# An inference step with attention scores as three float32r products, attention steps in pairs and later table requests

## Chip, cores and metric

The kernel runs on one core of a Trainium2 chip. The metric is the device time of one execution in microseconds (us). It is given as the median of several executions, and one further execution was recorded by the profiler. TensorE does the matrix products, VectorE (DVE), ScalarE (ACT) and GpSimd (POOL) the elementwise work. SyncE (SP) requests most transfers, GpSimd's queue requests the attention tables.

## The reference

One step of a two-layer model on 128 context tokens and 256 latent tokens (a grid of 4 rows by 64), model width 1024. Each layer, cut to its lines:

```python
h = rmsnorm(x, g1) * (1 + sc1) + sh1
u = h @ w_in
u_pool, u_q, u_k, u_v, u_x, u_y, u_g = jnp.split(u, SPLITS, axis=-1)
y_a = pool_branch(u_pool, pool_w, pool_scale)
y_b = attn_fn(q, k, v).reshape(b, l, ATTN_W)
hf, hb = rglru_branch(u_x, conv_w, conv_b, wa, ba, wx, bx, lam, h0f, h0b)
y_c = (hf + hb) * gelu(u_y)
proj = einsum('blnw,nwd->blnd', stack([y_a, y_b, y_c]), w_branch)
x = x + gt1 * (sum(gates * proj) @ w_out)
x = x + gt2 * ((silu(fg) * fu) @ w_ff_out)
```

Attention has 8 heads of 64. A context query sees the 128 context keys. A latent query has one softmax over its grid neighbourhood, with a learned bias and a column mask, together with 128 cached context keys:

```python
s_lat = einsum(qg, kb) * ATTN_SCALE + bias
s_lat = jnp.where(mask, s_lat, NEG_INF)
s_ctx = einsum(qg, ck) * ATTN_SCALE
p = softmax(concatenate([s_lat, s_ctx]))
```

The shifts, scales and gates come from SiLU(cond) @ w_mod + b_mod, six vectors of 1024 per layer (the modulation).

## The kernel before

All 384 tokens are the columns of every large product. Every large operand is split into two float32r halves, hi = round(x) and lo = x - hi, and a product is the sum hi·hi + lo·hi + hi·lo (`mm3`, L340 to L344). ACT makes the hi half of a weight tile (L305), DVE the lo half (L314); an activation is split likewise by `split_g` (L359, L362) or `split_from`.

The program is one list of jobs written out by hand. A `job` (L408) takes its weight tiles, runs their products, calls `tick()` (which moves on the pending generators of earlier evacuations, among them those in `lazy`), calls `side_step()` (one step of a side branch) and pushes its own evacuation. `after()` then adds a rate `modr[0]` times the job's units and does one modulation step for each whole number reached (`mod_step`, one DVE product-and-sum of 128x1024, L262). The rates of layer l are the rows of `MR` (L49). The first three belong to the branches in the order in which they run, which are pool, LRU and attention (b = 0, 2, 1), the fourth to the stage between pool and LRU, in which `values_job` and `qkv(p)` for p = 0 to 3 make values, queries and keys.

Attention is a side branch (`branch_attn`, L691). Its units are (p, hh, qt): a pair of heads p, a head of the pair hh, and a query block qt of 128 latent queries; with qt = 0 come the 128 context queries as well. There are 16 units a layer. It is a loop over steps i, one step for each job: at even i the scores of two units (L702, two heads, each on 64 of the 128 rows of TensorE's array), at i + 1 the first part of the softmax (`soft_a`, whose DVE step is L718), then `soft_b`, `soft_c` (its DVE step is L735), transposes (L744), their copy out of PSUM (`evac`), and at odd i the products with the values of a pair of units (L774, L779). A score tile is three products in fp32: queries by 256 keys, by the 128 cached keys (`ckv`), and for qt = 0 the context queries by the context keys. `mask_bias` (L686) adds the column mask to the two bias tables of a pair, `load_attn` (L671) requests bias tables and cached keys and values for a pair, and `ev_qkv` (L846) moves queries and keys out of PSUM in fp32.

At the start of layer 0, `start()` (L935 to L1177) works on the first modulation vectors. Near its end `fb` products (L1157) are turned by seven small `mt` products (L1168) into the shift of the first tiles, whose evacuations go into `lazy`. The jobs 19 to 23 follow (job 19 makes the last LRU tile, 20 to 23 the gates `gy` of that branch), and then `pool_proj` (L583), four products of pooled tiles `pd` whose halves are `pdh` and `pdl`. The LRU tiles are `xp`, and their convolution `cv` has one ACT step (L596) and three DVE steps (L599).

Of the kernel before, what the change touches and what calls it, by code (L numbers as in the profile page):

```python
# [20 lines left out]
NT = NC_ + NL  # L21
# [24 lines left out]

WN = (8, 1, 1, 3)

MR = ((0.7, 2.3, 1.8, 0.3, 1.3, 1.1, 0.1), (0.6, 0.8, 0.8, 0.3, 1.3, 0.7, 0))  # L49


def chunk_order():
# [38 lines left out]
def emit(ctx, tc, A, outs):  # L91
# [594 lines left out]
    def mask_bias(y, p):  # L686
        for h in (2 * p, 2 * p + 1):
            t = y["bias", h][:, :384].rearrange("p (r c) -> p r c", r=6)
            V.tensor_tensor(t, t, cmask.unsqueeze(1).to_broadcast([128, 6, 64]), op=OP.add)

    def branch_attn(l, y):  # L691
        def scores(p, qt):

            ss = [psum("sc") for _ in range(2)]
            q, k, ck = y["q", p], y["k", p], y["ckv", p]
            parts = [(slice(0, 256), k, slice(128, 384), 128 + qt * 128), (slice(256, 384), ck, slice(0, 128), 128 + qt * 128)]
            if qt == 0:
                parts.append((slice(384, 512), k, slice(0, 128), 0))
            for o_, m, c_, qo in parts:
                for hh in range(2):  # L700
                    r = slice(64 * hh, 64 * hh + 64)
                    T.matmul(ss[hh][:, o_], q[r, qo:qo + 128], m[r, c_], start=True, stop=True)  # L702
            return ss

        def soft_a(s, h, qt):
            pr, m = heap("pr"), small("m")
            bo = 128 if qt == 0 else 0
            n = 2 if qt == 0 else 1
            prs = [pr, m]
            S.activation(pr[:, 256:384], s[:, 256:384], AF.Copy)  # L710
            if qt == 0:
                pc = heap("pc")
                S.activation(pc[:, :128], s[:, 384:512], AF.Copy)
                prs.append(pc)
            V.tensor_reduce(m[:, 0:n], s[:, 256:256 + n * 128].rearrange("p (a c) -> p a c", a=n),
                            axis=AX.X, op=OP.max)
            r4 = dict(r=4)
            V.tensor_tensor_reduce(pr[:, 0:256].rearrange("p (r c) -> p r c", **r4),  # L718
                                   s[:, 0:256].rearrange("p (r c) -> p r c", **r4),
                                   y["bias", h][:, bo:bo + 256].rearrange("p (r c) -> p r c", **r4)[:, :, ::-1],  # L720
                                   op0=OP.add, op1=OP.max, scale=1.0, scalar=m[:, 0:1], accum_out=m[:, 0:1])
            V.tensor_scalar(m[:, 2:2 + n], m[:, 0:n], -1.0, None, op0=OP.mult)
            return prs

        def soft_b(prs):
            m = prs[1]
            S.activation(prs[0][:, :384], prs[0][:, :384], AF.Exp, bias=m[:, 2:3], accum_out=m[:, 4:5])
            if len(prs) == 3:
                S.activation(prs[2][:, :128], prs[2][:, :128], AF.Exp, bias=m[:, 3:4], accum_out=m[:, 5:6])

        def soft_c(prs):
            n = len(prs) - 1
            m = prs[1]
            V.reciprocal(m[:, 6:6 + n], m[:, 4:4 + n])
            V.tensor_scalar(prs[0][:, :384], prs[0][:, :384], m[:, 6:7], None, op0=OP.mult)  # L735
            if n == 2:
                V.tensor_scalar(prs[2][:, :128], prs[2][:, :128], m[:, 7:8], None, op0=OP.mult)

        def transp(prs):
            tp = psum("tp")  # L740
            n = len(prs) + 1
            for j in range(n):
                src = prs[0][:, j * 128:(j + 1) * 128] if j < 3 else prs[2][:, :128]
                T.transpose(tp[:, j * 128:(j + 1) * 128], src, ident)  # L744
            return tp, n

        def evac(tp, n):
            pt = heap("pt")
            pts = [pt]
            S.activation(pt[:, :384], tp[:, :384], AF.Copy)  # L750
            if n == 4:
                pc = heap("ptc")
                V.tensor_copy(pc[:, :128], tp[:, 384:512])
                pts.append(pc)
            return pts

        units = [(p, hh, qt) for p in range(4) for qt in range(2) for hh in range(2)]
        pr, o, pend = {}, {}, []
        nu = len(units)

        def begin(p):
            mask_bias(y, p)

        def values(j):
            p, _, qt = units[2 * j]
            ts = [pr.pop(2 * j), pr.pop(2 * j + 1)]
            vv, cv = y["vv", p], y["ckv", p]
            if qt == 0:
                o[p] = psum("o")
            for jj in range(-1 if qt == 0 else 0, 3):  # L770
                for hh in range(2):
                    rows = slice(hh * 64, hh * 64 + 64)
                    if jj < 0:
                        T.matmul(o[p][rows, 0:128], vv[:, rows], ts[hh][1][:, 0:128], start=True, stop=True,  # L774
                                 skip_group_check=True)
                        continue
                    wv = cv[:, 128 + hh * 64:192 + hh * 64] if jj == 2 else \
                        vv[:, 128 * (jj + 1) + hh * 64:128 * (jj + 1) + hh * 64 + 64]
                    T.matmul(o[p][rows, 128 + qt * 128:256 + qt * 128], wv, ts[hh][0][:, jj * 128:(jj + 1) * 128],  # L779
                             start=jj == 0, stop=jj == 2, skip_group_check=True)  # L780

        i = 0
        while i < nu + 7 or pend:
            if i < nu and ("k", units[i][0]) not in y:
                yield
                continue
            for g in list(pend):
                if next(g, "end") == "end":
                    pend.remove(g)
            if 0 <= i - 1 < nu:  # L790
                p, hh, qt = units[i - 1]
                pr[i - 1] = soft_a(pr[i - 1], 2 * p + hh, qt)
            if 0 <= i - 2 < nu:
                soft_b(pr[i - 2])
            if 0 <= i - 3 < nu:
                soft_c(pr[i - 3])
            if 0 <= i - 5 < nu:
                pr[i - 5] = evac(*pr[i - 5])
            if i % 2 and 0 <= i - 7 < nu:
                values((i - 7) // 2)  # L800
            if 0 <= i - 4 < nu:
                pr[i - 4] = transp(pr[i - 4])
            if i % 2 == 0 and i < nu:
                p, hh, qt = units[i]
                if qt == 0:
                    begin(p)
                pr[i], pr[i + 1] = scores(p, qt)
            if i % 4 == 2 and 0 <= i - 10 < nu:
                p = (i - 10) // 4
                pend.append(split_g(putter(y, (1, p)), o.pop(p)[:, :NT], name="yb"))  # L810
                next(pend[-1])
                for key in (("vv", p), ("ckv", p), ("bias", 2 * p), ("bias", 2 * p + 1), ("q", p), ("k", p)):
                    y.pop(key)
            i += 1
            yield
# [29 lines left out]

    def ev_qkv(l, kind, p, y):  # L846
        def f(ps):
            t = heap(kind)
            S.activation(t[:, :NT], ps[:, :NT], AF.Copy, scale=0.125 if kind == "q" else 1.0)
            if kind != "q":  # L850
                G.dma_start(out=outs[kind][l, p], in_=t[:, 0:128])
            y[kind, p] = t
            return
            yield
        return f
# [79 lines left out]
    def start(y):  # L935
# [227 lines left out]
        for hf in range(3):  # L1163
            n = 384 if hf < 2 else 128
            S.activation(sb[hf][:, :n], fb[hf][:, :n], AF.Copy)
        ps = psum("mt")
        for g in range(7):
            T.matmul(ps[:, 2 * g:2 * g + 2], sb[g // 3][:, (g % 3) * 128:(g % 3) * 128 + 128], sel,  # L1168
                     start=True, stop=True)
        shw = cp.tile([128, 14], F32, name="shw0")  # L1170
        V.tensor_copy(shw, ps[:, 0:14])
        evs = [ev_pool(0, g, y) for g in range(4)] + [ev_ux(0, c, y) for c in range(3)]
        for g, ev in enumerate(evs):
            lazy.append(ev((un[g], shw[:, 2 * g:2 * g + 2])))
        load_crow()
        w_ahead(0)
        return mv  # L1177

    for l in range(L):
        y = {}  # L1180
        if l == 0:
            mv = start(y)
            todo = [19, 20, 21, 22, 23]
        else:
            mv = first_group(l, 1, [("in", l, m) for m in range(4)], [ev_pool(l, g, y) for g in range(4)], 2)
# [4 lines left out]
            job([[("in", l, m, 8)]], mv, ev, **kw)  # L1190

        for m in todo:
            win(m, ev_pool(l, m, y) if m < 4 else ev_ux(l, m - 16, y) if m < 20 else ev_uy(l, m - 20, y))
        def qkv(p):
            if p < 3:
                load_attn(l, y, p + 1)
            win(4 + p, ev_qkv(l, "q", p, y))
            win(8 + p, ev_qkv(l, "k", p, y))

# [190 lines left out]
```

## Time and profile before

| what | us |
|---|---|
| median of 3 executions | 1232.99 |
| lowest and highest | 1231.52, 1233.26 |
| the profiled execution | 1231.6 |
| its span, first to last instruction | 1229.8 |
| TensorE busy | 1219.8 |
| DVE busy | 888.3 |
| ACT busy | 598.4 |
| POOL busy | 72.6 |

Of the profiled execution 1.8 us lie around the span. The granted TensorE clock is 0.999 of full speed over the span. A busy time is the union of an engine's instructions, so a matrix product that has started but waits in the pipeline counts as well. The share of an engine is a mean over stages; the rows further on show single stages.

### The profile page before, as it was taken

To read this page: it belongs to the slowest core of one execution; us is meant where nothing else is said; L and a number is where in the kernel's file an instruction comes from. 1 tells how busy PE (TensorE), PEld (TensorE's weight loads), DVE (VectorE), ACT (ScalarE), POOL (GpSimd) and SP (SyncE) were. 2 spreads that over 40 slices of the span, in tenths; PEclk is the share of its full clock that TensorE was granted. 3 is DMA by queue.
4 is the path that set the end of the run, shared out by engine and by line. 5 is a ranking of instruction groups with operands and counts; after the bars stand their busy time and mean duration, and the time that the engine had idled before them with its cause. 6 is when DMAs were issued, how large, how long until landed. Compare 5 with 4: busy or idle time off the path is not lost.

```text
span 1229.8 us, 19387 instructions
## 1 busy us (share of the span) xinstructions
PE 1219.8 (99%) x7348; PEld 1190.6 (97%) x7348; DVE 888.3 (72%) x1650; ACT 598.4 (49%) x1103; POOL 72.6 (6%) x187
## 2 busy tenths in 40 slices
PE   9999999999999999999999999999999999999997
PEld 7799999899999999999999999999999999999997
DVE  6798698998978887757779668787676785442432
ACT  5587845544455333333357576564344743332321
POOL 0000150000200000010000013100010000000000
PEclk9999999999999999999999999999999999999999
DMA  9635684466626666645643457632553355333321
GB/s 346 256 132 190 187 177 134 147 209 217 202 98 207 235 226 212 202 150 182 214 138 113 158 167 190 142 118 100 172 197 129 119 207 171 131 109 108 115 88 52
DMA packets 63645, 204.30 MB, mean 166 GB/s; under 512 B 7744, under 2 KB 10944, under 8 KB 63424
## 3 DMA queue, kind: packets, MB, share of 16 engines
q1 hardware_dynamic: 60912, 197.56, 48.2%
q0 software_dynamic: 2496, 5.25, 3.5%
q8 instruction: 57, 0.93, 0.3%
q14 instruction: 36, 0.29, 0.1%
q10 hardware_dynamic: 144, 0.26, 0.1%
HBM read 200.41 MB, written 2.63 MB: 165 GB/s over the span
## 4 chain that ended last, share of the span: by engine, by line
PE 58%; issue 22%; DVE 1%; POOL 0%; POOLq 0%; DVEq 0%
PE ps L342 18%; PE ps L344 18%; PE ps L343 18%; PE tp L744 1%; PE o L779 1%; PE sc L702 1%; PE vt L1210 0%; PE vt L1211 0%; PE vt L1212 0%; DVE junk L262 0%; DVE wlo L314 0%; PE o L774 0%; DVE pr L718 0%; PE st L473 0%; DVE yo L1306 0%
## 5 line engine op out<-in xcount | busy, mean ns | idle before, releaser
L342 PE MATMUL ps<-hh,whi 128*128 128x384 f32 x1256 | 422.2, 336 | 0.0
L344 PE MATMUL ps<-hl,whi 128*128 128x384 f32 x1256 | 419.9, 334 | 0.0
L343 PE MATMUL ps<-hh,wlo 128*128 128x384 f32 x1256 | 419.7, 334 | 0.0
L314 DVE TENSOR_TENSOR wlo<-raw,whi 128x1024 fp32r<-128x1024 f32 (+2 forms) x296 | 322.8, 1115 | 21.7 <-ACT whi L305 21.7
L305 ACT ACTIVATE whi<-raw 128x1024 fp32r<-128x1024 f32 (+2 forms) x296 | 279.8, 970 | 97.3 <-PE ps L344 59.8
L342 PEld LDWEIGHTS ps<-hh,whi 128*128 128x128 f32 x1256 | 235.7, 188 | 2.4 <-issue 0.3
L343 PEld LDWEIGHTS ps<-hh,wlo 128*128 128x128 f32 x1256 | 235.8, 188 | 0.1
L344 PEld LDWEIGHTS ps<-hl,whi 128*128 128x128 f32 x1256 | 235.7, 188 | 0.0
L262 DVE SCALAR_TENSOR_TENSOR junk<-wm,crow 128x1024 bf16<-128x1024 f32 x160 | 195.4, 1221 | 27.0 <-DMA wm<-in_wm 25.0
L909 ACT ACTIVATE ft<-ps 128x384 f32<-128x384 f32 x40 | 19.7, 493 | 202.8 <-PE ps L344 202.8
L342 PE MATMUL ps<-svh,whi 128*128 128x384 f32 x352 | 117.6, 334 | 0.0
L343 PE MATMUL ps<-svh,wlo 128*128 128x384 f32 x352 | 117.6, 334 | 0.0
L344 PE MATMUL ps<-svl,whi 128*128 128x384 f32 x352 | 117.6, 334 | 0.0
L894 DVE SCALAR_TENSOR_TENSOR x<-ps,modv,x 128x128 f32<-128x128 f32 x64 | 23.7, 412 | 81.6 <-PE ps L344 81.5
L911 DVE TENSOR_TENSOR ft<-ft,ps 128x384 f32<-128x384 f32 x40 | 22.1, 552 | 80.7 <-ACT ft L909 80.7
L872 ACT ACTIVATE tg<-ps 128x384 f32<-128x384 f32 x48 | 23.4, 489 | 89.0 <-PE ps L344 88.2
L342 PEld LDWEIGHTS ps<-svh,whi 128*128 128x128 f32 x352 | 66.1, 188 | 0.0
L343 PEld LDWEIGHTS ps<-svh,wlo 128*128 128x128 f32 x352 | 66.1, 188 | 0.0
L344 PEld LDWEIGHTS ps<-svl,whi 128*128 128x128 f32 x352 | 66.1, 188 | 0.0
L881 DVE SCALAR_TENSOR_TENSOR tg<-tg,ps 128x384 f32<-128x384 f32 x48 | 26.4, 551 | 44.0 <-PE ps L344 43.9
L453 ACT ACTIVATE sq<-x 128x384 f32<-128x384 f32 x40 | 20.1, 513 | 66.4 <-DVE x L894 66.4
L342 PE MATMUL ps<-mgh,whi 128*128 128x384 f32 x128 | 42.8, 334 | 0.0
(242 smaller groups left out, 1770.7 us busy)
## 6 DMA issues: line engine op xcount, KB each, us to landing
raw<-in_fi SPq DMA_DIRECT2D x88, 512.0 KB, 4.3
raw<-in_in SPq DMA_DIRECT2D x82, 512.0 KB, 3.9
wm<-in_wm SPq DMA_DIRECT2D x80, 512.0 KB, 4.3
raw<-in_fo SPq DMA_DIRECT2D x32, 512.0 KB, 4.6
raw<-in_br SPq DMA_DIRECT2D x48, 256.0 KB, 2.7
w<-in_wm SPq DMA_DIRECT2D x16, 512.0 KB, 7.0
raw<-in_wo SPq DMA_DIRECT2D x16, 512.0 KB, 3.7
raw<-in_fo SPq DMA_DIRECT2D x16, 384.0 KB, 3.1
```

The costliest lines, as they stand in the source:

```text
L262: V.scalar_tensor_tensor(j, t, 0.5, crow[:, s], op0=OP.mult, op1=OP.mult, accum_out=modv[l][:, comp, d, s:s + 1])
L305: S.activation(hi[:, :nk], r[:, :nk], AF.Copy)
L314: V.tensor_tensor(lo[:, :nk], r[:, :nk], hi[:, :nk].bitcast(F32), op=OP.subtract)
L342: T.matmul(ps[:, :n], hi[:, k], mv[0][:, :n], start=start, stop=False)
L343: T.matmul(ps[:, :n], lo[:, k], mv[0][:, :n], start=False, stop=False)
L344: T.matmul(ps[:, :n], hi[:, k], mv[1][:, :n], start=False, stop=stop)
L453: S.activation(sq[:, :NT], xt[d], AF.Square)
L872: S.activation(t[:, :NT], ps[:, :NT], AF.Tanh, scale=0.5)
L881: V.scalar_tensor_tensor(t[:, :NT], t[:, :NT], 1.0, ps[:, :NT], op0=OP.add, op1=OP.mult)
L894: V.scalar_tensor_tensor(xt[d][:, o:o + n], ps[:, o:o + n], modv[l][:, comp, d, s:s + 1], xt[d][:, o:o + n], op0=OP.mult, op1=OP.add)
L909: S.activation(t[:, :NT], pg[:, :NT], AF.Silu)
L911: V.tensor_tensor(t[:, :NT], t[:, :NT], pu[:, :NT], op=OP.mult)
```

## The change

Five edits. The scores become three float32r products of query and key halves: `ev_qkv` splits queries and keys as they leave PSUM (and copies the context keys to a tile `ko` for the output), and `prep(p)` splits the cached keys on GpSimd into `ck`. The attention loop handles the two units of a pair together at an odd step, transposes, values and then scores, and copies both transposed tiles at an even step. The mask is added by GpSimd. Layer 0's modulation rates are other numbers. The tables of a pair are requested at that pair's predecessor's first scores and no longer in `qkv`, and the seven `mt` products with their evacuations (`rest()`) come one job later.

```diff
-MR = ((0.7, 2.3, 1.8, 0.3, 1.3, 1.1, 0.1), (0.6, 0.8, 0.8, 0.3, 1.3, 0.7, 0))
+MR = ((1.1, 1.9, 1.6, 0.5, 1.3, 1.1, 0.1), (0.6, 0.8, 0.8, 0.3, 1.3, 0.7, 0))
...
-            V.tensor_tensor(t, t, cmask.unsqueeze(1).to_broadcast([128, 6, 64]), op=OP.add)
+            G.tensor_tensor(t, t, cmask.unsqueeze(1).to_broadcast([128, 6, 64]), op=OP.add)
...
-            q, k, ck = y["q", p], y["k", p], y["ckv", p]
+            q, k, ck = y["q", p], y["k", p], y["ck", p]
...
-                for hh in range(2):
-                    r = slice(64 * hh, 64 * hh + 64)
-                    T.matmul(ss[hh][:, o_], q[r, qo:qo + 128], m[r, c_], start=True, stop=True)
+                for a, b in ((0, 0), (1, 0), (0, 1)):
+                    for hh in range(2):
+                        r = slice(64 * hh, 64 * hh + 64)
+                        T.matmul(ss[hh][:, o_], q[a][r, qo:qo + 128], m[b][r, c_], start=a + b == 0, stop=b == 1,
+                                 skip_group_check=True)
...
-        def begin(p):
+        def prep(p):
+
+            t, c = y["ckv", p], heap("ck", F32R)
+            hi, lo = c[:, 0:128], c[:, 128:256]
+            G.tensor_copy(hi, t[:, 0:128])
+            G.tensor_tensor(lo, t[:, 0:128], hi.bitcast(F32), op=OP.subtract)
+            y["ck", p] = (hi, lo)
             mask_bias(y, p)
...
+            if 0 <= i < nu:
+                p, hh, qt = units[i]
+                pr[i] = soft_a(pr[i], 2 * p + hh, qt)
             if 0 <= i - 1 < nu:
-                p, hh, qt = units[i - 1]
-                pr[i - 1] = soft_a(pr[i - 1], 2 * p + hh, qt)
+                soft_b(pr[i - 1])
             if 0 <= i - 2 < nu:
-                soft_b(pr[i - 2])
...
+                soft_c(pr[i - 2])
+            if i % 2 == 0:
+                for u in (i - 6, i - 5):
+                    if 0 <= u < nu:
+                        pr[u] = evac(*pr[u])
+            else:
+                for u in (i - 5, i - 4):
+                    if 0 <= u < nu:
+                        pr[u] = transp(pr[u])
+                if 0 <= i - 7 < nu:
+                    values((i - 7) // 2)
+                if i + 1 < nu:
+                    p, hh, qt = units[i + 1]
+                    if qt == 0 and p < 3:
+                        load_attn(l, y, p + 1)
+                    pr[i + 1], pr[i + 2] = scores(p, qt)
+            if i % 4 == 2 and i < nu and units[i][0] < 3:
+                prep(units[i][0] + 1)
...
-            t = heap(kind)
-            S.activation(t[:, :NT], ps[:, :NT], AF.Copy, scale=0.125 if kind == "q" else 1.0)
-            if kind != "q":
-                G.dma_start(out=outs[kind][l, p], in_=t[:, 0:128])
-            y[kind, p] = t
+            if kind == "k":
+                t = heap("ko")
+                S.activation(t[:, 0:128], ps[:, 0:128], AF.Copy)
+                G.dma_start(out=outs["k"][l, p], in_=t[:, 0:128])
+            y[kind, p] = split_from(ps[:, :NT], scale=0.125 if kind == "q" else 1.0, name=kind)
...
-        ps = psum("mt")
-        for g in range(7):
-            T.matmul(ps[:, 2 * g:2 * g + 2], sb[g // 3][:, (g % 3) * 128:(g % 3) * 128 + 128], sel,
-                     start=True, stop=True)
...
+        def rest():
+            ps = psum("mt")
+            for g in range(7):
+                T.matmul(ps[:, 2 * g:2 * g + 2], sb[g // 3][:, (g % 3) * 128:(g % 3) * 128 + 128], sel,
+                         start=True, stop=True)
...
+            for g, ev in enumerate(evs):
+                lazy.append(ev((un[g], shw[:, 2 * g:2 * g + 2])))
...
+            if m == 20 and l == 0:
+                rest()
...
-            if p < 3:
-                load_attn(l, y, p + 1)
```

TensorE's order at one place of the attention of layer 0, before: the values of a pair run behind a job together with three transposes, and scores follow a job later behind four transposes (`tp`: transposes, `o`: values, `sc`: scores, `ps`: the big products of a job).

```order
L774 MATMUL o<-ptc,vv 64x128 x2
L779 MATMUL o<-pt,vv 64x128 x4
L779 MATMUL o<-pt,ckv 64x128 x2
L744 MATMUL tp<-ident,pr 128x128 x3
L342 MATMUL ps<-ych,whi 128x384
...
L344 MATMUL ps<-ycl,whi 128x384
L744 MATMUL tp<-ident,pr 128x128 x3
L744 MATMUL tp<-ident,pc 128x128
L702 MATMUL sc<-k,q 128x256 x2
L702 MATMUL sc<-ckv,q 128x128 x2
L702 MATMUL sc<-k,q 128x128 x2
```

After, at the place where the same pair's values stand (`kh`, `kl`, `qh`, `ql` are the halves of keys and queries, `ck` those of the cached keys):

```order
L748 MATMUL tp<-ident,pr 128x128 x6
L784 MATMUL o<-ptc,vv 64x128 x2
L789 MATMUL o<-pt,vv 64x128 x4
L789 MATMUL o<-pt,ckv 64x128 x2
L703 MATMUL sc<-kh,qh 128x256 x2
L703 MATMUL sc<-kh,ql 128x256 x2
L703 MATMUL sc<-kl,qh 128x256 x2
L703 MATMUL sc<-ck,qh 128x128 x2
L703 MATMUL sc<-ck,ql 128x128 x2
L703 MATMUL sc<-ck,qh 128x128 x2
L703 MATMUL sc<-kh,qh 128x128 x2
L703 MATMUL sc<-kh,ql 128x128 x2
```

The transposes of two units, the values of a pair and the scores of the next pair now form one block between two jobs, and each score product is there three times. Over a layer there are 19 such blocks of small products before and 12 after.

ACT's order ahead of `pool_proj` in layer 0, before: the hi halves of the last two pooled tiles (`pdh`) stand on either side of the first LRU tile (`xp`, `cv`) and of the last gate (`gy`, job 23).

```order
L305 ACTIVATE whi<-raw 128x1024
L359 ACTIVATE pdh<-pd 128x384
L559 ACTIVATE xp<-un,shw_863 128x128
L559 ACTIVATE xp<-un,shw_863 128x256
L596 ACTIVATE cv<-xp,par 128x386
L840 ACTIVATE gy<-ps 128x384
L359 ACTIVATE pdh<-pd 128x384
```

And after:

```order
L858 ACTIVATE gy<-ps 128x384
L359 ACTIVATE pdh<-pd 128x384
L559 ACTIVATE xp<-un,shw_935 128x128
L559 ACTIVATE xp<-un,shw_935 128x256
L596 ACTIVATE cv<-xp,par 128x386
L359 ACTIVATE pdh<-pd 128x384
```

The last gate now stands ahead of both hi halves, and the whole stretch of the first LRU tile between the two. On DVE the three steps of that tile's convolution stand ahead of the lo half of the last pooled tile, before as after.

## Rows read from the trace of the kernel before

**Rows 1.** The page, part 1: busy us, share of the span, instructions

```profile
PE 1219.8 (99%) x7348; PEld 1190.6 (97%) x7348; DVE 888.3 (72%) x1650; ACT 598.4 (49%) x1103; POOL 72.6 (6%) x187
```

**Rows 2.** TensorE's waits: waiting line, released by, us, times, longest

```profile
PE mt L1168 <- ACT mb L1165: 1.0, 1, 1.0
PE tp L744 <- DVE pr L735: 0.6, 1, 0.6
```

**Rows 3.** Timeline of TensorE in a job of layer 0: start us, us

```profile
68.73 0.33 PE L343 MATMUL ps<-hh,wlo 128*128 128x384 f32 x1
...
71.33 0.33 PE L343 MATMUL ps<-hh,wlo 128*128 128x384 f32 x1
```

**Rows 4.** Timeline of TensorE around one block of scores, layer 1

```profile
764.55 0.34 PE L344 MATMUL ps<-hl,whi 128*128 128x384 f32 x1
764.81 0.70 PE L702 MATMUL sc<-k,q 64*128 64x256 f32 x4
765.35 0.39 PE L702 MATMUL sc<-ckv,q 64*128 64x128 f32 x4
765.57 0.39 PE L702 MATMUL sc<-k,q 64*128 64x128 f32 x4
765.89 0.44 PE L342 MATMUL ps<-hh,whi 128*128 128x384 f32 x1
766.17 0.34 PE L343 MATMUL ps<-hh,wlo 128*128 128x384 f32 x1
```

**Rows 5.** Timeline of TensorE at the `mt` products

```profile
56.49 1.72 PE L1168 MATMUL mt<-sel,mb 128*128 128x2 f32 x14 [1.02 <-ACT mb L1165]
58.07 0.42 PE L342 MATMUL ps<-hh,whi 128*128 128x384 f32 x1
```

**Rows 6.** Timeline of TensorE at transposes, layer 1

```profile
783.70 0.49 PE L744 MATMUL tp<-ident,pr 128*128 128x128 f32 x3
784.03 0.27 PE L744 MATMUL tp<-ident,pc 128*128 128x128 f32 x1
```

**Rows 7.** Timeline of ACT ahead of the pool products, layer 0

```profile
79.16 0.49 ACT L840 ACTIVATE gy<-ps 128x384 f32<-128x384 f32 x1 [0.81 <-PE ps L344]
79.55 0.52 ACT L359 ACTIVATE pdh<-pd 128x384 fp32r<-128x384 f32 x1
79.96 0.80 ACT L559 ACTIVATE xp<-un,shw 128x128 f32<-128x128 f32 x2
80.85 0.71 ACT L596 ACTIVATE cv<-xp,par 128x386 f32<-128x386 f32 x1
```

**Rows 8.** Timeline of DVE in the same stretch

```profile
80.30 0.55 DVE L362 TENSOR_TENSOR pdl<-pd,pdh 128x384 fp32r<-128x384 f32 x1
81.59 2.00 DVE L599 SCALAR_TENSOR_TENSOR cv<-xp,par,cv 128x386 f32<-128x386 f32 x3 [0.74 <-ACT cv L596]
83.51 0.55 DVE L362 TENSOR_TENSOR xcl<-cv,xch 128x386 fp32r<-128x386 f32 x1
```

**Rows 9.** Timeline of TensorE, the last pool product

```profile
80.91 0.44 PE L344 MATMUL ps<-pdl,whi 128*128 128x384 f32 x1
```

**Rows 10.** Windows: us, PE, PEld, DVE, ACT, POOL busy (instructions), clock, DMA share, GB/s

```profile
204.00:264.00 60.00, 59.40 (x433) 54.65 (x431) 57.81 (x145) 32.70 (x84) 0.00 (x0) 1.00 0.48 154
798.00:860.00 62.00, 62.00 (x451) 57.11 (x450) 47.15 (x123) 32.37 (x85) 0.00 (x0) 1.00 0.35 115
```

**Rows 11.** Timeline of TensorE and DVE in one attention step, layer 0

```profile
216.49 0.38 PE L744 MATMUL tp<-ident,pr 128*128 128x128 f32 x2
219.24 0.48 DVE L718 CUSTOM_DVE_ANT_1 pr<-sc,bias,m 128x256 f32<-128x256 f32 x1
```

**Rows 12.** Groups of DVE instructions: count, busy us, mean ns, idle before

```profile
L262 DVE SCALAR_TENSOR_TENSOR junk<-wm,crow 128x1024 bf16<-128x1024 f32 x160 | 195.4, 1221 | 27.0 <-DMA wm<-in_wm 25.0
L689 DVE TENSOR_TENSOR bias<-bias,cmask 128x384 f32<-128x384 f32 x16 | 8.1, 550 | 0.0
```

**Rows 13.** Groups of POOL instructions, as above

```profile
L448 POOL TENSOR_TENSOR xsl<-modv,xsh 128x2 fp32r<-128x2 f32 x24 | 12.7, 529 | 70.5 <-DVE sq L458 52.3 <-PE ps L343 13.2 <-PE ps L344 2.6
```

**Rows 14.** Transfers: issuing queue, count, KB each, median us to landing

```profile
bias<-in_rpb POOLq DMA_DIRECT2D x32, 96.0 KB, 7.4
```

More of the change, by code (lines that the diff above doesn't have):

```diff
@@ L711, in soft_a @@
             if qt == 0:
-                pc = heap("pc")
+                if h % 2 == 0:
+                    y["pc", h // 2] = heap("pc")
+                pc = y["pc", h // 2][:, 128 * (h % 2):128 * (h % 2) + 128]
                 S.activation(pc[:, :128], s[:, 384:512], AF.Copy)
@@ L780, in values @@
                              start=jj == 0, stop=jj == 2, skip_group_check=True)
-        i = 0
+        prep(0)
+        i = -1
         while i < nu + 7 or pend:
-            if i < nu and ("k", units[i][0]) not in y:
+            if i % 2 and i + 1 < nu and ("k", units[i + 1][0]) not in y:
                 yield
@@ L789, in branch_attn @@
                     pend.remove(g)
+            if 0 <= i < nu:
+                p, hh, qt = units[i]
+                pr[i] = soft_a(pr[i], 2 * p + hh, qt)
             if 0 <= i - 1 < nu:
-                p, hh, qt = units[i - 1]
-                pr[i - 1] = soft_a(pr[i - 1], 2 * p + hh, qt)
+                soft_b(pr[i - 1])
             if 0 <= i - 2 < nu:
-                soft_b(pr[i - 2])
[L795 to L807, printed above, removed]
+                soft_c(pr[i - 2])
[16 more added lines that the diff above has]
+                prep(units[i][0] + 1)
             if i % 4 == 2 and 0 <= i - 10 < nu:
@@ L811, in branch_attn @@
                 next(pend[-1])
-                for key in (("vv", p), ("ckv", p), ("bias", 2 * p), ("bias", 2 * p + 1), ("q", p), ("k", p)):
+                for key in (("vv", p), ("ckv", p), ("ck", p), ("bias", 2 * p), ("bias", 2 * p + 1), ("q", p), ("k", p)):
                     y.pop(key)
@@ L1165, in start @@
             S.activation(sb[hf][:, :n], fb[hf][:, :n], AF.Copy)
-        ps = psum("mt")
-        for g in range(7):
-            T.matmul(ps[:, 2 * g:2 * g + 2], sb[g // 3][:, (g % 3) * 128:(g % 3) * 128 + 128], sel,
-                     start=True, stop=True)
[L1170 to L1174, printed above, removed]
+        def rest():
[3 more added lines that the diff above has]
+                         start=True, stop=True)
+            shw = cp.tile([128, 14], F32, name="shw0")
+            V.tensor_copy(shw, ps[:, 0:14])
+            evs = [ev_pool(0, g, y) for g in range(4)] + [ev_ux(0, c, y) for c in range(3)]
+            for g, ev in enumerate(evs):
+                lazy.append(ev((un[g], shw[:, 2 * g:2 * g + 2])))
         load_crow()
         w_ahead(0)
-        return mv
+        return mv, rest
     for l in range(L):
@@ L1181, in emit @@
         if l == 0:
-            mv = start(y)
+            mv, rest = start(y)
             todo = [19, 20, 21, 22, 23]
```

## The prediction

> **What bounds the kernel now.** I read the page's engine shares first, then the list of what TensorE waits for, then the timeline of its blocks of small matmuls, then DVE and ACT at the two places where the change moves their work. TensorE is busy 1219.8 us [rows 1] of the 1229.8 us span, and its waits on other engines come to about 3.5 us in all, of which only two concern this change: 1.0 us for `mb` ahead of the `mt` matmuls, and 0.6 us for one softmax tile [rows 2]. So a saving on ACT, DVE or POOL is worth at most those two waits. The time moves by what TensorE itself executes, and by new waits of TensorE. The unit of the big work is one product of 128x128 by 384 columns: 15 pitches from 68.73 to 71.33 [rows 3] make 0.173 us each, and they follow each other without a gap.
>
> **Scores, as they stand.** One block of a qt = 0 pair [rows 4] goes: the last big product starts at 764.55, so the next would start at 764.72; the scores start at 764.81 (0.09 later), the 256-column part takes 764.81 to 765.35, each 128-column part about 0.22, then the first big product starts at 765.89 and the second at 766.17 instead of 0.173 after it. The "x4" are two heads times two passes of fp32. The heads run side by side (each on 64 rows of the array), so I count passes, not records: two passes of 256 columns, 0.43; two of 128 columns, 0.218, twice; 0.86 us in all. The rest of the 1.275 us that the block puts between two big products, 0.42 us, is entry and exit: 0.09 to empty the array and 0.107 (0.28 − 0.173 at the end, and as much at the start) for a weight load that nothing hides, each time the array changes its shape. A qt = 1 pair has one 128-column part less: 0.65 us.
>
> **Scores, as they will be.** Each part becomes three products of one pass: hi·hi, lo·hi, hi·lo, each with its own 128 columns of weights. No float32r product of under 384 columns runs before, so I bound its price from both sides.
> - At one column per cycle (0.417 ns at the 2.4 GHz level, which is granted: clock 1.00 in [rows 10]) the 384-column pitch of 0.173 shrinks by 128 x 0.417 ns = 0.053 to 0.12 for 256 columns, and by as much again to 0.066 for 128.
> - A weight load has a floor: 14 two-column records from 56.49 to 58.07 take 0.113 each [rows 5], and three transposes from 783.70 to 784.03 0.11 each [rows 6]. If it holds here, a 128-column product costs 0.11 too. qt = 0: 3 x 0.12 + 6 x 0.11 = 1.02 against 0.86; qt = 1: 0.36 + 0.33 = 0.69 against 0.65. Four pairs of each per layer: 4 x (0.16 + 0.04) = 0.8, in two layers **+1.6 us**. I take this value.
> - Lower bound, without that floor: qt = 0 0.36 + 0.40 = 0.76, qt = 1 0.36 + 0.20 = 0.56, thus 4 x (−0.10 − 0.09) = −0.76 a layer, −1.5 us.
> - Upper bound: 128-column products run at the pace of the fp32 ones [rows 4], 0.218 each: qt = 0 0.36 + 6 x 0.218 = 1.67, qt = 1 1.01, thus 4 x (0.81 + 0.36) = 4.7 a layer, +9.4 us.
>
> The rows with the floor are all of 128 partitions, and the score products use 64. The Trainium skill ("TensorE: Matmul & The Clock Gate", section LDWEIGHTS) says that a load takes its columns over 1.2 in ns, whatever the number of rows: 107 ns here, and the term by it is the +1.6 above; were a load of half the rows half as long, the term would be the −1.5. The 0.28 − 0.173 = 0.107 of [rows 4] agrees for 128 rows; no run here yet shows it for 64. It speaks against this change, since the third product costs a third load however few columns it has.
>
> **Pairs.** TensorE meets 19 small blocks a layer before and 12 after (the order of the attention rows). Counting shape changes in both orders gives four fewer a layer (four value blocks now run straight into scores): 4 x 0.2 = 0.8 us at most, 0 at least. Of this I keep a little over half, 0.45 a layer, since the blocks that merge had begun or ended with transposes, which share the big products' shape and so paid less at the joint: **−0.9 us**.
>
> **The start.** `rest()` puts the `mt` matmuls behind job 19, 24 products later, by when `mb` is long there: the wait of 1.02 us goes [rows 5]. Big products then stand on both sides of `mt`, so one more weight load of 0.11 lies open: −0.9. But the evacuations that `rest()` hands to `lazy` start one job later, and that has a price further on. ACT's order before is pdh(2), xp(0), cv(0), gy(23), pdh(3); after, gy(23), pdh(2), xp(0), cv(0), pdh(3). On DVE conv(0) x3 stands ahead of pdl(3) in both. Before, the sequence gy, pdh, xp, cv already runs, for the next tile and channel, at 79.16, 79.55, 79.96 and 80.85 [rows 7], and DVE's three conv steps for it from 81.59 on; the step behind them starts at 83.51 [rows 8]. After, that stretch carries tile 2 and channel 0 instead, and the step behind the conv steps is pdl(3), 0.55: it lands at 84.06 instead of 80.85. TensorE's last pool product, which reads it, starts at 80.91 [rows 9]; it would start near 84.1: a new wait of **+3.2 us**, with all big products behind it. (All these times come 0.9 earlier together, which the −0.9 has counted.) The start in all: −0.9 + 3.2 = **+2.3 us**. Bounds: −0.9 if pdl(3) is in time, +3.2 if the first wait is only moved and not lost.
>
> **DVE in layer 0.** DVE is busy 57.8 of 60 us at 204 to 264, against 47.2 of 62 us at the same place of layer 1 [rows 10]. There the softmax of a unit runs late: a block of TensorE starts at 216.49, its softmax step L718 for that block's unit only at 219.24 [rows 11]. In the new order the second transpose buffer of an odd step waits for a softmax of the same step, so such lateness turns into TensorE's wait. Against it: DVE loses 16 mask additions of 0.55 and, by the new rates, about 0.4 modulation steps of 1.22 [rows 12] a unit in the LRU branch (eight units) and 0.2 in attention; it gains sixteen lo halves of q and k of about 0.55 (as pdl in [rows 8]) and 0.2 steps a unit in the qkv stage (twelve units), 0.4 in pool. In 204 to 264, which holds the eight LRU units and some two masks, that is 8 x 0.4 x 1.22 + 1.1, about −5 us of 57.8, so I let the 0.6 us wait go and one of 0.8 come: **+0.2 us**; bounds −0.8 and +6 (three late steps of 2).
>
> **Costed at nothing.** The mask on POOL: POOL does nothing at all from 204 to 264 [rows 10]; its own two-input step takes 0.53 for two columns [rows 13], so at even five times DVE's 0.55 a unit's mask is done in its step of about 4 us; without that cover two masks of 2.7 would stand before each pair's softmax. The ck halves stand with it. Tables requested later: they land 7.4 us after issue [rows 14] and are needed four steps on, some 15 us. The copy `ko` on ACT, 0.3 eight times: ACT is busy 49%.
>
> **Sum.** 1.6 − 0.9 + 2.3 + 0.2 = +3.2 us. The profiled execution took 1231.6, thus 1234.8; it lies 1.4 under the median of the three runs, so the forecast is 1232.99 + 3.2 = **1236.2 us**. A measurement of this kernel tells about 0.2% (2.5 us) from no change; the three runs span 1.7.
>
> **Rivals.**
> - *Short products at fp32's pace* (the upper bound above). For it: nothing before shows a float32r product under 384 columns at any pace. Against: 384 columns do run at a column per cycle [rows 3]. 1236.2 + 9.4 − 1.6 = 1244.0 us.
> - *The heads lose their overlap*, each product waiting for the other head's load: qt = 0 3 x 0.24 + 12 x 0.11 = 2.04, qt = 1 1.38, so 4 x (1.18 + 0.73) = 7.6 a layer, +15.3. Against it are the fp32 heads of [rows 4], which do overlap. 1236.2 + 13.7 = 1249.9 us. The Trainium skill ("TensorEngine Tiling (Array Packing)", section Key Properties) says that different tiles load and multiply in parallel, which stands against this rival; the overlap in [rows 4] agrees for fp32, no run shows it for float32r.
> - *The softmax is late.* In layer 0 three odd steps wait 2 us each instead of 0.2 in all: +5.8, 1242.0 us. For it [rows 11], against it the freed DVE time.
> - *Not slower: the pool stall does not come.* If pdl(3) lands within about 0.7 us of the last pool product, the start gains its −0.9 instead of losing 2.3, and the sum is 0.0: 1233.0 us. It decides from there: each us by which pdh(2), cv(0) or the conv steps come earlier than I put them is a us less. Reason for it: gy(23) itself comes earlier once the `mt` wait is gone. Against it: TensorE comes earlier by the same amount. With the lower bound for short products on top, 1229.9.
>
> **How the numbers follow.** Forecast 0.44 (its own range 1233.5 to 1239), fp32's pace 0.23, overlap lost 0.07, late softmax 0.08, no pool stall 0.18. The range reaches up over fp32's pace and down past the case without a stall: 1231.5 to 1246; outside it are the lost overlap and the ends of the others, under 0.2. Slower by over 0.2% means over 1235.5: two thirds of the forecast's own range (0.29) and the three dear cases (0.38): 0.67. Faster, under 1230.5, only with both lower ends: 0.05. Same: 0.28.
>
> **What would show it.** Right: TensorE no longer waits for `mb`; it waits about 3 us for `pdl` at the last pool product, near 80 us; a qt = 0 score block alone takes about 1.44 instead of 1.275, starts of its 128-column products 0.11 apart; 24 instead of 38 blocks; POOL masks of 0.5 to 2.7 us that nobody waits for. Wrong: pitches of 0.22 or twice 0.11 in the score block, a wait of `tp` for L718's tiles in 200 to 260, or no wait for `pdl`.

## The result and the profile after

The changed kernel takes 1248.38 us (median of four runs, 1247.93 to 1253.82), against 1232.26 before in the same comparison: 1.0141 times the time, interval 1.0127 to 1.0154. (Ratios here and below are those of the comparison and not quotients of the two medians, which here give 1.0131.) It is 16 us slower where 3.2 were forecast, and outside the range.

The engine shares of the changed kernel, which answer to [rows 1]:

```profile
span 1246.0 us, 19621 instructions
PE 1225.4 (98%) x7428; PEld 1197.9 (96%) x7428; DVE 894.0 (72%) x1650; ACT 598.3 (48%) x1111; POOL 97.8 (8%) x219
```

TensorE is busy 5.6 us longer, but the span is 16.2 us longer: most of the loss is idle time of TensorE. TensorE's list of waits, which answers to [rows 2] (waiting line, released by: us in all, times, longest):

```profile
PE o L784 <- DVE ptc L757: 4.3, 3, 3.2
PE tp L748 <- DVE m L722: 3.8, 3, 1.4
PE ps L344 <- DVE pdl L362: 1.5, 1, 1.5
PE warm L1068 <- POOL ident masks.py:199: 1.4, 1, 1.4
PE o L789 <- ACT pt L754: 0.9, 2, 0.5
PE ps L342 <- ACT pdh L359: 0.9, 1, 0.9
PE sc L703 <- DVE kl L351: 0.6, 1, 0.6
PE ps L342 <- ACT xsh L440: 0.5, 1, 0.5
```

The wait for `mb` is gone and one for `pdl` has come, as forecast; that for `pdh` was not forecast. New are 9.6 us in attention blocks (`o`, `tp`, `sc`), of which the prediction had 0.8. To place the loss I set the start of the same big product (they are the same 6360 in both kernels) beside each other in the two traces. The changed kernel is 1.9 us behind after the pool products, 2.9 after the first scores, 11.1 after the attention of layer 0, 11.2 when that of layer 1 begins and 16.2 when it has ended; nothing is added after that. So: start 1.9, first scores 1.0, attention 8.1 and 5.0.

The costliest stall, in the timeline of TensorE in layer 0:

```profile
208.48 0.82 PE L748 MATMUL tp<-ident,pr 128*128 128x128 f32 x6
212.55 0.52 PE L784 MATMUL o<-ptc,vv 128*64 128x128 f32 x3 [3.25 <-DVE ptc L757]
```

The block begins on time with its six transposes, and then the value products want `ptc`, the copy that DVE makes of transposes of the block before. DVE is late by 3.25 us. Going back along DVE leads to a softmax step that waited for ACT, and ACT's timeline 12 us earlier shows where the delay began:

```profile
195.71 0.28 ACT L712 ACTIVATE pr<-sc 128x128 f32<-128x128 f32 x1 [1.04 <-issue]
200.63 0.28 ACT L717 ACTIVATE pc<-sc 128x128 f32<-128x128 f32 x1 [4.64 <-PE tp L748]
200.81 0.61 ACT L731 ACTIVATE pr<-pr,m 128x384 f32<-128x384 f32 x1
```

L717 copies a score tile that has long been there. It has no use for a transpose, and yet it waits 4.64 us for one, the one at the head of TensorE's next block. A wait on a reader of other data means a place in memory: `pc` is to be put where `pr` of an earlier unit lies until it has been transposed. Everything behind it on ACT and, through the softmax, on DVE stands still, and when the next block comes DVE has a backlog.

The working tiles (`heap`) have 60 places. Counting, in the order in which the program issues its instructions, how many are held at a time, from first write to last read, gives 62 at the most before and 65 after. Queries and keys now hold four tiles a pair instead of two, and the cached keys' halves one more. In the kernel before four or five tiles a layer take a place whose last read is issued later than their own first write, by 2 to 11 instructions; in the changed one fifteen do, by 10 to 51. `pc` above is the first of them: the read that it waits for is issued 51 instructions behind it.

### The profile page after: what moved, and what is told of

It reads as the page before. It is cut to its first block, busy times and chain, and to the rows that moved or that the text cites. A ratio compares the mean times of both kernels' runs of the same rounds, so it can differ in the third digit from the quotient of the medians.

```text
span 1246.0 us, 19621 instructions
## 1 busy us (share of the span) xinstructions
PE 1225.4 (98%) x7428; PEld 1197.9 (96%) x7428; DVE 894.0 (72%) x1650; ACT 598.3 (48%) x1111; POOL 97.8 (8%) x219
## 4 chain that ended last, share of the span: by engine, by line
PE 70%; issue 22%; DVE 3%; DMA 2%; POOL 1%; ACT 1%; POOLq 0%; DVEq 0%; ACTq 0%
PE ps L342 21%; PE ps L344 21%; PE ps L343 21%; DMA bias<-in_rpb 1%; PE o L789 1%; DMA ckv<-in_ckv 1%; PE sc L703 1%; PE vt L1232 1%; PE vt L1230 1%; PE vt L1231 1%; PE tp L748 1%; PE ma L976 1%; DVE wlo L314 0%; POOL bias L689 0%; POOL bias L680 0%
## 5 line engine op out<-in xcount | busy, mean ns | idle before, releaser
L442 POOL CAST xsh<-modv 128x2 fp32r<-128x2 f32 x24 | 12.5, 520 | 387.8 <-DVE modv L270 205.8
```

## The experiments

Twelve kernels, in three sets; each was compared with the kernel before on the same chip, which took 1233.19, 1232.88 and 1231.66 us. Theory 1 is the shortage of places; the rivals are GpSimd's masks and the later tables (2) and DVE's load in layer 0 (3), the late-softmax case of the prediction.

**More places, narrower tiles.** Nothing but the tile's width, alignment and number:

```diff
-HW_ = 448
+HW_ = 416
-    hp = ctx.enter_context(tc.tile_pool(name="hp", bufs=60))
+    hp = ctx.enter_context(tc.tile_pool(name="hp", bufs=66))
-        return hp.tile([128, HW_], dt, name=name, tag="t", align_bytes=256)
+        return hp.tile([128, HW_], dt, name=name, tag="t", align_bytes=128)
```

> The changed kernel with 66 working tiles of 416 columns in place of 60 of 448; nothing else changes. Theory 1 (the working tiles run out: halves of q, k and the cached keys make the demand 65, so new tiles of the softmax take places that are still read by transposes or values of a later block, and TensorE then waits in the attention of both layers): the attention waits (about 8.1 us in layer 0 and 5.0 in layer 1) nearly vanish and the half-clock stretch of layer 0 with them; left are about 1.9 at the start and 1 at the first scores, so about 1236 us. Theory 2 (the masks and cached-key halves on GpSimd and the later tables are late): tiles don't matter, within 2 us of 1248. Theory 3 (DVE is late in layer 0, as in the prediction): layer 0 keeps its 8 us, about 1243.

The same on the kernel before:

> The kernel before with 66 tiles of 416 columns. Theory 1: its demand is 62 and its waits on tiles are hidden but for at most the 0.6 us, so 1232 us or up to 1 less. A faster result by more than 2 us would say that the narrower tiles help by themselves.

Measured: changed 1245.79 us, 1.0105 (1.0089 to 1.0121); before 1243.59 us, 1.0081 (1.0064 to 1.0098). The second was a surprise: narrow tiles alone cost 10 us (below, under the hardware). But between these two, with the same tiles, the change costs 2.2 us (the difference of the medians) and not 16. The waits of TensorE in the changed kernel with 66 tiles:

```profile
PE ps L344 <- DVE pdl L362: 1.5, 1, 1.5
PE warm L1068 <- POOL ident masks.py:199: 1.4, 1, 1.4
PE ps L342 <- ACT pdh L359: 0.9, 1, 0.9
PE ps L342 <- ACT xsh L440: 0.5, 1, 0.5
PE ma L988 <- DVE lp L203: 0.2, 1, 0.2
```

No attention wait is left in either layer, with scores, masks, tables and rates as changed. The block that had stalled, in its timeline:

```profile
210.62 0.82 PE L748 MATMUL tp<-ident,pr 128*128 128x128 f32 x6
211.37 0.44 PE L784 MATMUL o<-ptc,vv 128*64 128x128 f32 x4
```

**Places of the old width.** One raw weight buffer fewer (`NR` 5 for 6) pays for 63 tiles:

> The changed kernel with 63 working tiles of the old width and alignment, paid for by one raw weight buffer fewer (5 for 6). Theory 1 (too few tiles): the demand of 65 exceeds the places by at most 2 instead of 5, so most attention waits of 8.1 and 5.0 us go, and no product gets slower as with the 416-column tiles: 1235 to 1239 us, unless the smaller weight ring makes waits of its own. If the waits stay at 1246 to 1249, tiles of the old width don't help and theory 1 falls.

Measured: 1250.61 us, 1.0150 (1.0133 to 1.0167). By what I had written down theory 1 would fall here, for the time stayed where it was. I was wrong in counting places only: the wait of `tp` falls from 3.8 to 0.6 us, but `o` now waits 7.8 us for `ptc`. ACT's timeline shows why:

```profile
207.41 0.28 ACT L712 ACTIVATE pr<-sc 128x128 f32<-128x128 f32 x1 [8.88 <-DMA out_k<-ko]
```

With other places, a score copy falls on that of `ko`, the copy of the keys for the output, and waits until its transfer has left. How many places lack matters less than whose place is taken: only four tiles a layer take a place too early here, instead of fifteen, and the loss is no smaller. (The kernel before was not run with `NR` 5; TensorE waits for no split weight in this trace.) So I gave as many as are ever held, 65, at the price of one pair of split weight tiles (`NH` 5 for 6), and the same to the kernel before:

> The changed kernel with 65 working tiles of the old width, paid for by 5 instead of 6 pairs of split weight tiles; 65 is the largest demand, so no tile has to wait for a place. Theory 1: no attention waits; 1.9 at the start and up to 1 at the first scores are left, so 1234 to 1237, shifted by what the same cut costs the kernel before (the next run). Theory 1 is wrong, or not the whole, if o, tp or sc still wait for DVE by several us.

> Control: the kernel before with 65 tiles and 5 pairs of split weight tiles. 1233 if the cut costs nothing; it may cost some us by making ACT and DVE start a weight's split later.

Measured: changed 1259.64 us, 1.0221 (1.0207 to 1.0235); before 1259.78, 1.0221 (1.0205 to 1.0236). The cut itself costs 28 us, far more than I had allowed for, so the absolute forecast of the first missed; the two then take the same time. The changed kernel's waits on DVE and ACT are now mainly those for split weights, as in the control, and none of `o`, `tp` or `sc` is left. First the changed kernel:

```profile
PE ps L343 <- DVE wlo L314: 11.2, 9, 1.7
PE ps L342 <- ACT whi L305: 5.2, 2, 2.6
PE ps L344 <- DVE pdl L362: 1.5, 1, 1.5
```

and the control:

```profile
PE ps L343 <- DVE wlo L314: 14.0, 11, 1.7
PE ps L342 <- ACT whi L305: 5.2, 2, 2.6
```

Since the control waits 2.8 us longer for weights, the equal times do not say that the change is free; that is read from the 2.2 us above. What this pair shows is the list: with 65 places the attention's waits are gone.

**Less demand.** Scores in fp32 again, so that the halves of queries, keys and cached keys and the copy `ko` go; pairs, GpSimd's masks, later tables, rates and the moved start stay. 60 tiles are held at the most:

```diff
-            q, k, ck = y["q", p], y["k", p], y["ck", p]
+            q, k, ck = y["q", p], y["k", p], y["ckv", p]
...
-                for a, b in ((0, 0), (1, 0), (0, 1)):
-                    for hh in range(2):
...
+                for hh in range(2):
+                    r = slice(64 * hh, 64 * hh + 64)
+                    T.matmul(ss[hh][:, o_], q[r, qo:qo + 128], m[r, c_], start=True, stop=True)
...
-            y[kind, p] = split_from(ps[:, :NT], scale=0.125 if kind == "q" else 1.0, name=kind)
+            y[kind, p] = t
```

> The changed kernel with scores in fp32 again (no halves of q, k or cached keys, no extra copy of k for the output); pairs, mask on GpSimd, rates, table requests and the start stay changed. The demand is then 60 tiles, as many as there are. Theory 1: no attention waits at all; left are 1.9 at the start and about -0.5 to -1 for fewer blocks, 1233.5 to 1235. Theory 2 (late masks or tables) or 3 (DVE late): these edits are still in, so the attention waits stay for the most part, 1242 and more.

Measured: 1232.70 us, 1.0002 (0.9993 to 1.0011), a little better than expected, with no wait of `o`, `tp` or `sc`. Masks on GpSimd and late tables are still in: as the cause theory 2 falls.

**A shortage in the kernel before.** Places 58 for 60, nothing else:

> The kernel before with 58 tiles for a demand of 62, nothing else: new tiles of the softmax then wait for transposes and scores of blocks that are still to come, as in the changed kernel. Theory 1: attention waits of TensorE in both layers, several us, 1237 to 1250, with unchanged scores, steps, masks and tables. Without them theory 1 has nothing that shows it by itself.

Measured: 1236.60 us, 1.0040 (1.0027 to 1.0054), just under the forecast range. Its waits:

```profile
PE tp L744 <- DVE pr L735: 3.0, 2, 1.5
...
PE o L774 <- DVE ptc L753: 0.9, 2, 0.5
```

The waits of the changed kernel come up with none of its edits, smaller (in the trace it falls behind by 2.2 us, then 2.5 in layer 0, of which 1.6 are a stretch at half clock, and 0.9 in layer 1). Twelve tiles a layer take a place too early here, but most of them wait for a read that is issued at most 16 instructions behind, where in the changed kernel most are over 30 behind.

**Single edits.** The mask back on VectorE (`G.tensor_tensor` to `V.tensor_tensor` in `mask_bias`):

> The changed kernel with the column mask on VectorE again. Theory 1: places of tiles are taken at the same steps, so the attention's waits stay, 1246 to 1249 us. Theory 2: the mask of 2 us a pair on GpSimd, and the DVE steps that slow down beside it, are the cause: 1238 to 1242.

Measured: 1254.81 us, 1.0178 (1.0163 to 1.0193): 6 us worse than the changed kernel, outside the figures of both theories. Its waits:

```profile
PE o L784 <- DVE ptc L757: 3.1, 3, 2.1
PE tp L748 <- DVE m L722: 2.7, 2, 1.3
PE sc L703 <- ACT kh L349: 2.5, 1, 2.5
```

In its trace all that it loses against the changed kernel's has been lost before the first stall of the attention: 1.2 us in a stretch at half clock near 84, 3.7 at the first scores, where TensorE waits for `kh` (ACT had waited 3.78 us for DVE just before it), and 1.8 at half clock behind that. The attention's own waits of `o` and `tp` are 6.7 us, against 9.0 in the changed kernel, and the longest is 2.1 instead of 3.2. So the masks on GpSimd may lengthen the stalls (theory 2 may have a small part; the delay ahead of them gives DVE time as well), but the stalls do not go with the masks. The old rates of layer 0:

> The changed kernel with the old modulation rates of layer 0. Theory 1: rates move DVE's steps in layer 0 only and no tile; within 3 us of 1248 either way, and layer 1's 5 us stay. Theory 3 (DVE late in layer 0): the new rates relieve the LRU branch, so undoing them makes layer 0 worse, 1251 and more.

Measured: 1253.15 us, 1.0173 (1.0159 to 1.0187), 5 us worse. In the trace, which is 4.3 us longer, 2.4 of that are a stretch at half clock behind the start; layer 0's attention loses 2.3 more and the first scores 0.9 less. So DVE's load does matter (theory 3), but only as the size of a backlog: with 66 places neither layer of the changed kernel waits for it. The `mt` products at their old place:

> The changed kernel with the mt products and their evacuations where they were before. If the start costs what the traces show (1.9 us later at the pool products), it takes about 1246.5 us, and the waits for pdh and pdl go while that for mb comes back; the attention waits stay. If the attention's waits hang on the order of the start: far from that.

Measured: 1248.79 us, 1.0130 (1.0111 to 1.0148). This tells nothing on the start: its four runs spread over 5 us (1246.89 to 1252.08). The waits did move as said (`pdh` and `pdl` gone, 1.0 for `mb` back). So the start was put alone on the kernel before:

> The kernel before with the mt products and their evacuations one job later, alone. By the trace of the changed kernel the start loses 1.9 us net (a wait of 2.4 for the halves of the pooled tiles, less 1.0 for mb, and rests): 1235 us. By the rival, in which the start is even: 1233.

Measured: 1234.73 us in 11 runs, 1.0015 (1.0006 to 1.0024): +1.9 us, with an interval of 0.7 to 3.0. The 1.9 of the changed kernel's trace lies in it, but that they agree to a tenth is luck: the trace of this run is 1.8 behind at the pool products and loses 1.6 more in a stretch at half clock right behind them, which the changed kernel's trace does not have.

**What is left that helps.** fp32 scores with the start as before:

> The changed kernel with fp32 scores and with the mt products at their old place: left of the change are the pairs, the mask on GpSimd, the rates and the later table requests. The start alone measured +1.9 us, fp32 scores with the moved start -0.2 against before: so about 1230.8 us, 0.15% under before. If the wait for the halves of the pooled tiles was hiding something, 1232 to 1233.

Measured: 1230.79 us in 11 runs, 0.9985 (0.9977 to 0.9994). This is the fastest of these kernels: pairs, masks on GpSimd, rates and later tables gain 0.9 us when the halves and the moved start are left out.

## Why the prediction was wrong

**The step that failed** is "costed at nothing" together with the softmax rival. I costed the halves of queries, keys and cached keys as instructions on DVE, ACT and POOL, and never as tiles that are held. Before, 62 tiles for 60 places was already over the edge, and [rows 2] had a trace of it: the 0.6 us of `tp` on `pr`, which I put down to DVE's load ([rows 10, 11]) alone. With 65 the changed kernel loses 8.1 us in layer 0 and 5.0 in layer 1. That layer 1 stalls too speaks against DVE's load as the cause, since DVE had 15 us to spare there [rows 10]; that it all goes with 66 or 65 places, or with fp32 scores, shows the cause. The late-softmax rival had the right symptom (TensorE waits for the softmax at odd steps) and 8% at 5.8 us, with the wrong origin and in one layer only.

**Start: right.** Forecast +2.3; measured 1.9 in the trace, and 1.9 (0.7 to 3.0) alone. The two rows on which it hung, in the timelines of TensorE and DVE of the changed kernel:

```profile
80.74 0.44 PE L342 MATMUL ps<-pdh,whi 128*128 128x384 f32 x1 [0.87 <-ACT pdh L359]
82.84 0.45 PE L344 MATMUL ps<-pdl,whi 128*128 128x384 f32 x1 [1.49 <-DVE pdl L362]
```

```profile
80.31 2.00 DVE L599 SCALAR_TENSOR_TENSOR cv<-xp,par,cv 128x386 f32<-128x386 f32 x3 [0.93 <-ACT cv L596]
82.23 0.55 DVE L362 TENSOR_TENSOR pdl<-pd,pdh 128x384 fp32r<-128x384 f32 x1
```

The lo half stands behind the three convolution steps, as read from ACT's order and [rows 7, 8]. The waits come to 2.4 us; from the products ahead of them to those behind, the lag against the kernel before goes from −1.3 to +1.9, which is the 3.2 of the forecast. The hi half `pdh` waits too, which I had not seen, so the wait for `pdl` is 1.5 and not 3.2.

**Scores: right in kind, half the size.** Forecast +1.6. The prices per product came out as forecast but for one; the timeline of one block of the changed kernel with 66 tiles:

```profile
212.39 0.39 PE L703 MATMUL sc<-kh,qh 64*128 64x256 f32 x2
212.61 0.28 PE L703 MATMUL sc<-kh,ql 64*128 64x256 f32 x2
212.73 0.28 PE L703 MATMUL sc<-kl,qh 64*128 64x256 f32 x2
212.85 0.22 PE L703 MATMUL sc<-ck,qh 64*128 64x128 f32 x2
212.91 0.27 PE L703 MATMUL sc<-ck,ql 64*128 64x128 f32 x2
213.02 0.28 PE L703 MATMUL sc<-ck,qh 64*128 64x128 f32 x2
213.13 0.27 PE L703 MATMUL sc<-kh,qh 64*128 64x128 f32 x2
```

From start to start it is 0.12 with 256 columns and 0.11 with 128, as forecast, but once 0.06, and this 0.05 in each of sixteen blocks is what I had too much; why that one is shorter stays open. Alone, a qt = 0 block takes 1.38 us (forecast 1.44, [rows 4] 1.275), a qt = 1 block 1.04 (1.055 before): 4 x (0.10 − 0.01) twice, +0.7 us. The rule of the Trainium skill ("TensorE: Matmul & The Clock Gate", section LDWEIGHTS), that a load of 64 rows takes as long as one of 128, agrees with the 0.11. The heads overlap: x2 in one row is two heads, and the next row starts 0.11 or 0.12 after it.

**First scores: missed, 1.0 us.** The first block of layer 0 waits 0.6 us for `kl` and 0.2 for `kh`. With 66 places, and with the old rates alone, its cost is the undisturbed 1.37 to 1.38, so places and DVE's load both have a part; how the two act together stays open.

**Pairs: right.** Forecast −0.9; with fp32 scores the twelve blocks of a layer sum to 23.6 us (each from the last big product before it to the second after it, less two pitches) against 24.05 for the nineteen: −1.0 in all.

**DVE: near the lower bound.** With fp32 scores or 66 places the 0.6 us wait goes and nothing comes. It also goes in the kernel before when that has 66 places, so it was a wait for a place from the start. **Masks and tables on POOL: right.** A mask takes 1.1 us on POOL instead of 0.55 and TensorE has no wait for it; that it slows DVE beside it (last section) was not in the sum and tells only where DVE has a backlog. Without a shortage on either side the terms sum to 1.9 + 0.7 − 1.0 = +1.6, against the 2.2 measured between the two kernels with 66 places.

## What to carry to other kernels

Cost a split operand as space too: count how many tiles are held at the worst step and compare it with the places, before and after, and look whose place a new tile takes, for the count alone did not give the price here (four tiles a layer that come too early cost as much as fifteen). Do so even if the program still fits, since a shortage shows up as order and not as an error. In a trace its sign is an instruction that waits for a reader of data it does not touch (here a copy of scores for a transpose). Such a wait also holds up what stands behind it on its engine, as the 4.64 us on ACT did, so the place where time is lost lies a block later and under another name.

## What the hardware showed besides

**Where a tile begins matters to TensorE.** With tiles of 1664 bytes at multiples of 128 the kernel before took 10 us more, with no new wait on the tiles; many of its big products are a little slower. Sorted by the address of the moving tile, which the compiled program has, the mean pitch from start to start in that run is 174.0 ns at a multiple of 256 bytes and 176.8 at an odd multiple of 128, some 2900 products of each; in the changed kernel with 66 tiles it is 173.8 and 176.9. In the kernel before all tiles begin at multiples of 256, and the mean is 173.5. The 2.8 ns on 2900 products make 8 of the 10 us. Width and number of the tiles are the same for both kinds within a run, so the address is the likely cause; no run changed it alone.

**The clock fell behind some waits.** Windows of the changed kernel (us, PE, PEld, DVE, ACT, POOL busy, granted clock, DMA share, GB/s):

```profile
210.00:212.00 2.00, 0.00 (x0) 0.00 (x0) 1.93 (x6) 0.49 (x1) 2.00 (x3) 1.00 0.75 225
222.00:224.00 2.00, 0.63 (x4) 0.42 (x4) 1.68 (x7) 0.82 (x4) 0.00 (x0) 1.00 0.63 202
226.00:228.00 2.00, 2.00 (x15) 1.66 (x14) 0.29 (x1) 2.00 (x5) 0.07 (x1) 0.50 0.48 170
228.00:230.00 2.00, 2.00 (x7) 2.00 (x7) 1.71 (x6) 1.49 (x7) 1.92 (x4) 0.50 0.01 4
```

After idle stretches at 210 and 222 the clock is granted at 0.50 (the 1.2 GHz level) from about 225 to 232: 7 products in 2 us where 0.173 a piece makes 11.5. By an estimate, half of the busy time in that stretch, about 3 of layer 0's 8.1 us in this trace are this; but two of the kernel's other runs were granted 0.998 of the clock over the span instead of this one's 0.996, and took no less time (1248.49 and 1248.27 us against 1247.93). In layer 1, with similar waits, it stays at 1.00. At the start it is as uneven. The start moved alone, behind its wait for `pdl`:

```profile
84.00:86.00 2.00, 2.00 (x8) 2.00 (x8) 1.96 (x4) 1.64 (x5) 0.00 (x0) 0.50 0.00 0
```

Five of the eight traces with the moved start have such a stretch there, the changed kernel's own does not; of the six with the old start four have one behind the wait for `mb`, the kernel before does not. A difference of 1.6 us between two single traces can be this alone.

**DVE is slower beside GpSimd.** In the timelines of DVE and POOL of the changed kernel:

```profile
211.28 1.01 DVE L741 TENSOR_SCALAR pc<-pc,m 128x128 f32<-128x128 f32 x1
```

```profile
210.16 2.05 POOL L689 TENSOR_TENSOR bias<-bias,cmask 128x384 f32<-128x384 f32 x2
```

Alone L741 takes 0.28. The Trainium skill ("SBUF — State Buffer", section Who interferes with whom, on the shared port pair) says that some DVE operations and GpSimd's exclude each other for a whole instruction; this row agrees, since L741 ends at 212.29 and the two masks at 212.21, while the softmax step L722 keeps its 0.48 beside a mask. Here it lengthened the backlog before the 3.25 us stall by about 1 (0.7 at this step, 0.4 at the one before it), and with the masks on VectorE the longest such wait was 2.1.
